# Odd mixer's entry: decays moved to GpSimd and ahead of the first MLP, input sums that scale one addend themselves, rows of values in a lasting pool

## The chip, the cores and the metric

The kernel runs on one core of one Trainium2 chip. The metric is device time in microseconds (us) of one execution, the median of several runs. Engines are called as in the profile: PE (TensorE matmul), PEld (its weight load), DVE (VectorE), ACT (ScalarE), POOL (GpSimd), SP (SyncE, which issues DMAs here).

## What is computed

Two layers of an encoder on 512 tokens of 1024 columns, float32. Layer 0 is an even mixer (windowed and neighbourhood attention) and an MLP, layer 1 an odd mixer (retention) and an MLP. Cut to what matters:

```python
def _odd_mixer(x, norm_g, w_in, dec_f, dec_b, gn_g, w_out):
    h = _rmsnorm(x, norm_g)
    q, k, v, g = _split(h @ w_in, ODD_SPLITS)
    ...
    lgf = jax.nn.log_sigmoid(dec_f.astype(jnp.float32))
    lgb = jax.nn.log_sigmoid(dec_b.astype(jnp.float32))
    y_f = _retention_dir(q, k, v, lgf, False)
    y_b = jnp.flip(_retention_dir(jnp.flip(q, 1), jnp.flip(k, 1), jnp.flip(v, 1), lgb, True), 1)
    ...  # group norm of y_f + y_b
    return (jax.nn.silu(g) * yn) @ w_out

def _mlp(x, norm_g, w1, w2):
    h = _rmsnorm(x, norm_g)
    return jnp.square(jax.nn.relu(h @ w1)) @ w2

x = x + _even_mixer(x, ...);  x = x + _mlp(x, mlp_norm[0], ...)
x = x + _odd_mixer(x, ...);   x = x + _mlp(x, mlp_norm[1], ...)
```

The retention of each of eight heads weights a pair of tokens by a decay, exp(lg * distance), where lg is the logarithm of a sigmoid of one learned number per head and direction: 16 numbers in all.

## The kernel before

Every product is made of three float32r products: each operand is split into a high part (a cast on ACT: `xh`, `whi`, `shi`, `uh`, `qh`, `ath`) and a low part (a subtraction on DVE: `xl`, `wlo`, `slo`, `ul`, `ql`, `atl`), and PE adds high-high, high-low and low-high. The activations stand transposed, eight tiles `xT[0..7]` of 128 columns of x by 512 tokens.

The stages follow each other on PE: the even mixer (to about 222 us), the first MLP, the odd mixer, the second MLP. The MLPs' products and the odd mixer's values go through a seven-product scheme (class `Strassen`, and `Values` derived from it). Before these products, `combine(i)`, four times a stage, makes four sums out of two tiles of x: both tiles are scaled by the norm's gains on ACT (tiles `y`), four DVE operations of 128x256 make the sums in a tile `c` (L1003 to L1006), ACT casts them to `uh` (L1009) and DVE subtracts to `ul` (L1010). In the odd mixer `c` has one buffer.

What sets the order: within the steps of the seven-product scheme (`stream`) the order on PE, ACT and DVE is the written one. Elsewhere, and always on POOL and SP, a scheduler in the compiler orders each engine's instructions: in program order where possible, a later instruction earlier when its inputs and its memory are there. Each engine then works in that order and waits where an input is late. Memory is taken from pools; a pool that is opened where an earlier one was closed waits for the earlier one's readers and writers.

The odd mixer's entry, in the code's order:

- `leave` (end of the first MLP): x is transposed back on PE into PSUM, ACT and DVE make the high and low parts `xh`, `xl`, and the eight tiles are copied from PSUM to `xT` (L1357), five by DVE and three by ACT.
- 25 DVE operations on 128x16 and one ACT exponential (L1588 to L1603) compute `lg` and `nlb`, the decays, from `hb`, a tile loaded in the even mixer (L520). Their tiles lie in a pool of the odd mixer. `gn` (L1606) scales the group norm's gains.
- `project` of the first quarter: q, then the four `combine` calls among k (L1679, L1684 scale them), with weights through `load_w` (L138 load, L159 high, L160 low).
- `values.stream()`: 28 steps of products (L1487 to L1489). `take`, `give`, `scale`, `centre` (L1522 to L1546) turn them into rows (tiles `s` in the pool `odd_values`, six buffers). The first quarter's rows are split at once, the other twelve are stored to DRAM on SP (L1713) and loaded again later into tiles `vr` (L1707).
- Then the pool `odd_late` is opened on the memory of the closed `odd_values`, and the heads begin: `tmp` (L1746) is the product of scores and decays, `ath` and `atl` (L1640, L1641) its parts, multiplied with the values in L1754 to L1756.

Block sums of weights come from DMAs: SP loads one block, POOL issues a second DMA that adds the other (L1064, tiles `sraw`). POOL also does a few operations of the even mixer: `qn` (L451, L456), `nb` (L751), some `wlo` (L160).

Of the kernel before, what the change touches and what calls it, by code (L numbers as in the profile page):

```python
# [9 lines left out]
F32 = mybir.dt.float32  # L10
F32R = mybir.dt.float32r
AF = mybir.ActivationFunctionType
ALU = mybir.AluOpType
# [3 lines left out]
P = 128  # L17
S = 512
# [9 lines left out]
V_ATTN, V_RET, V_MLP, V_GN, V_QA, V_KA, V_QB, V_KB = 0, 8, 16, 32, 48, 49, 50, 51  # L28
# [4 lines left out]
def hybrid_encoder_kernel(  # L33
# [18 lines left out]
    nc = tc.nc  # L52
    mm = nc.tensor.matmul
    act = nc.scalar.activation
# [37 lines left out]
    tok_ss = consts.tile([P, NB, 2], F32, name="tok_ss")  # L92
    tok_v = consts.tile([P, NB], F32, name="tok_v")
    tok_r = consts.tile([P, 2, NB], F32, name="tok_r")

    consts.tile([P, 64], F32, name="filler")


    def after(ins, before):
# [210 lines left out]
    class Norm:  # L310


        def __init__(self, vec):
            self.vec = vec
            self.xg = new_xg()

        def gain(self, d):
            return gv[:, self.vec + d : self.vec + d + 1]

        def add(self, d):  # L320
            split_gain(self.xg[d], xT[d], self.gain(d))
# [630 lines left out]
    class Strassen:  # L952
# [37 lines left out]
        def combine(self, i):  # L990

            pool, norm = self.pool, self.norm
            y = []
            for m in range(2):
                d = 2 * i + m
                t = pool.tile([P, S], F32, tag="s", bufs=self.SB, name="y")
                act(t, xT[d], AF.Copy, scale=gv[:, norm.vec + d : norm.vec + d + 1])
                y.append(t)
            b11, b12 = y[0][:, :256], y[0][:, 256:]
            b21, b22 = y[1][:, :256], y[1][:, 256:]  # L1000
            tag, bufs = self.CB
            c = pool.tile([P, 4, 256], F32, tag=tag, bufs=bufs, name="c")
            V.tensor_tensor(c[:, 0], b11, b12, op=ALU.subtract)  # L1003
            V.scalar_tensor_tensor(c[:, 1], c[:, 0], -1.0, b22, op0=ALU.mult, op1=ALU.subtract)
            V.tensor_tensor(c[:, 2], b22, b12, op=ALU.subtract)
            V.scalar_tensor_tensor(c[:, 3], c[:, 1], -1.0, b21, op0=ALU.mult, op1=ALU.subtract)  # L1006
            h = pool.tile([P, 4, 256], F32R, tag=f"uh{i}", name="uh")
            l = pool.tile([P, 4, 256], F32R, tag=f"ul{i}", name="ul")
            nc.scalar.copy(h, c)  # L1009
            V.tensor_tensor(l, c, h[:].bitcast(F32), op=ALU.subtract)  # L1010
            (xh0, xl0), (xh1, xl1) = norm.xg[2 * i], norm.xg[2 * i + 1]
            self.ins[i] = {
                "B11": (xh0[:, :256], xl0[:, :256]),
                "B21": (xh1[:, :256], xl1[:, :256]),
                "B22": (xh1[:, 256:], xl1[:, 256:]),
                "U1": (h[:, 0], l[:, 0]),
                "U2": (h[:, 1], l[:, 1]),
                "T3": (h[:, 2], l[:, 2]),
                "T4": (h[:, 3], l[:, 3]),
            }  # L1020
# [325 lines left out]
        def leave(self):  # L1346

            norm = self.next_norm()

            def split(part, ds):  # L1350
                for d in ds:
                    part(norm.xg[d], self.turned[d], norm.gain(d))

            def keep(ds, copy=V.tensor_copy):
                for d in ds:
                    xT[d] = resid.tile([P, S], F32, tag=f"xT{d}", name=f"xT{d}")
                    copy(xT[d], self.turned[d])  # L1357

            self.back(0)
            split(high_gain, range(4))  # L1360
            for d in range(2):
                split(low_gain, (d,))
                keep((d,))
            for t in (2, 3):
                self.square(t, 0, self.tmp())
            yield
            split(low_gain, (2, 3))
            for t in range(2):
                self.square(t, 1, self.tmp())
            self.back(1)  # L1370
            split(high_gain, range(4, 8))
            split(low_gain, range(4, 8))
            keep((2, 3, 4), nc.scalar.copy)
            keep((5, 6, 7))

        def scales(self):

# [64 lines left out]
    class Values(Strassen):  # L1442
# [1 line left out]

        SB = 6
        CB = ("c", 1)

        def __init__(self, pool, tiny, w, norm, done):  # L1450
            self.pool, self.tiny, self.w, self.norm, self.done = pool, tiny, w, norm, done
            self.raw, self.parts, self.ins, self.rows, self.ps = {}, {}, {}, {}, {}
            self.early, self.mid, self.post, self.asked = ({} for _ in range(4))
            self.steps = [(2, q, j, x) for q in range(2) for j in range(7) for x in range(2)]
            self.base = {(2, 0): 0, (2, 1): 14}
            self.requests()
# [113 lines left out]
                    f()  # L1570


    def odd_mixer(norm, next_norm):
        es = ExitStack()
        pool = es.enter_context(tc.tile_pool(name="odd", bufs=1))
        tiny = es.enter_context(tc.tile_pool(name="odd_tiny", bufs=1))
        tiny.tile([P, 24], F32, name="filler")
        late, marks = [], []
        scr = [None] + [dram.tile([S, S], F32, name=f"values{i}") for i in range(1, 4)]


        dx = hb[:, 8:24]
        n = 16
        lg = tiny.tile([P, n], F32, name="lg")
        u = tiny.tile([P, n], F32, name="ls_u")
        s2 = tiny.tile([P, n], F32, name="ls_s2")
        pl = tiny.tile([P, n], F32, name="ls_p")
        V.tensor_scalar(u, dx, -1.0, None, op0=ALU.mult)  # L1588
        V.tensor_tensor(u, u, dx, op=ALU.min)
        act(u, u, AF.Exp)  # L1590
        V.tensor_scalar(s2, u, 2.0, None, op0=ALU.add)
        V.reciprocal(s2, s2)
        V.tensor_tensor(u, u, s2, op=ALU.mult)
        V.tensor_tensor(s2, u, u, op=ALU.mult)
        V.tensor_scalar(pl, s2, 1.0 / 17, 1.0 / 15, op0=ALU.mult, op1=ALU.add)
        for c in (13, 11, 9, 7, 5, 3, 1):
            V.tensor_tensor(pl, pl, s2, op=ALU.mult)
            V.tensor_scalar(pl, pl, 1.0 / c, None, op0=ALU.add)
        V.tensor_tensor(pl, pl, u, op=ALU.mult)
        V.tensor_scalar(u, dx, 0.0, None, op0=ALU.min)  # L1600
        V.scalar_tensor_tensor(lg, pl, -2.0, u, op0=ALU.mult, op1=ALU.add)
        nlb = tiny.tile([P, 8], F32, name="nlb")
        V.tensor_scalar(nlb, lg[:, 8:16], -1.0, None, op0=ALU.mult)  # L1603

        gn = tiny.tile([P, 16], F32, name="gn")
        V.tensor_scalar(gn, gv[:, V_GN : V_GN + 16], -1.0 / 512, None, op0=ALU.mult)  # L1606
        gn_eps = tiny.tile([P, 1], F32, name="gn_eps")
        G.memset(gn_eps, GN_EPS)

# [33 lines left out]

        def tmp(bufs=3):
            return pool.tile([P, S], F32, tag="tmp", bufs=bufs, name="tmp")

        table = {"load": [], "exp": [], "silu": []}

# [16 lines left out]
        class Quarter:  # L1665
# [7 lines left out]
            def project(self):  # L1673
                qt = self.qt
                self.q, self.k = [None] * 2, [None] * 2

                def ev_q(m, ps):
                    t = tmp()
                    V.tensor_tensor(t, ps, rb, op=ALU.mult)  # L1679
                    self.q[m] = split(t, "q", 2)  # L1680

                def ev_k(m, ps):
                    t = tmp()
                    V.scalar_tensor_tensor(  # L1684
                        t, ps, float(np.float32(P**-0.5)), rb, op0=ALU.mult, op1=ALU.mult
                    )
                    self.k[m] = split(t, "k", 2)

                hook = None if qt else deviations
                mark = marks[-1] if qt else None  # L1690
                proj_a(w_in_o, 0, 8, qt * 256, xg, ev_q, hook)
                if qt == 0:
                    values.combine(0)
                    values.ask(-99, -2)
                    values.combine(1)
                    values.combine(2)
                    values.combine(3)
                proj_a(w_in_o, 0, 8, 1024 + qt * 256, xg, ev_k)
                if qt == 0:
                    values.scales(rc)  # L1700
                    values.ask(-2, 0)
                    values.enter()
                    return
                for t in range(NB):
                    r = late[0].tile([P, S], F32, tag="vr", bufs=4, name="vr")
                    with tc.issue_after(mark):
                        nc.scalar.dma_start(r, scr[qt][t * P : (t + 1) * P, :])  # L1707
                    self.v[t] = split(r, "v", 4)
# [110 lines left out]
        quarters = [Quarter(i) for i in range(4)]  # L1819
        with tc.tile_pool(name="odd_values", bufs=1) as first:  # L1820
            values = Values(
                first, tiny, w_in_o, norm, lambda q, t, row: quarters[q].keep_v(t, row)
            )
            quarters[0].project()
            for hl in range(2):
# [3 lines left out]
                values.stream()  # L1829
        late.append(es.enter_context(tc.tile_pool(name="odd_late", bufs=1)))  # L1830

        late[0].tile([P, 3232], F32, name="filler")
        for i in range(4):
            q, p = quarters[i], quarters[i - 1] if i else None
            n = quarters[i + 1] if i < 3 else None
# [35 lines left out]
                st.stream()  # L1871

    even_mixer(n_mlp0)
    mlp(0, n_mlp0(), n_odd)
    odd_mixer(n_odd(), n_mlp1)
    mlp(1, n_mlp1(), None)
# [79 lines left out]
```

## Time and profile before

| | |
|---|---|
| median of 3 runs | 1297.4 us (1297.08 to 1297.44) |
| profiled execution | 1296.8 us, its span 1295.0 us |
| PE / PEld busy | 1276.7 us (99%) / 1105.2 us (85%) |
| DVE / ACT / POOL busy | 1029.2 us (79%) / 818.7 us (63%) / 135.1 us (10%) |
| granted PE clock | 0.999 |
| chain that ended last | PE 88%, DVE 6%, ACT 3%, DMA 1% |

A row of a timeline has the start and the duration in us, the engine, the line, the operation, output<-inputs, shapes, and in brackets the engine's idle time before it with what ended that. A row of groups has busy us and mean ns of one, then the idle time before. A row of waits has who waited, for whom, the total, how often and the longest. Times are us from the span's start.

### The profile page before, as it was taken

What the parts mean: (1) busy time and instruction counts of PE and PEld (TensorE: products, weight loads), DVE (VectorE), ACT (ScalarE), POOL (GpSimd) and SP (SyncE); (2) the same over time, 40 slices, a digit from 0 to 9 for tenths busy, and PEclk for the clock granted to TensorE, in tenths of its full rate; (3) what the DMA queues carried; (4) which work ended last, traced back from release to release, by engine and by line L of the source; (5) the groups of instructions that cost most, each with busy time, mean ns of one, the idle gap of its engine ahead of it and who ended that gap; (6) DMA issues with size and microseconds to landing.
All of it is one profiled execution on the core that took longest, in us unless ns stands there. A gap on an engine that the chain in (4) does not pass through costs nothing.

```text
span 1295.0 us, 18645 instructions
## 1 busy us (share of the span) xinstructions
PE 1276.7 (99%) x6898; PEld 1105.2 (85%) x6898; DVE 1029.2 (79%) x1596; ACT 818.7 (63%) x1369; POOL 135.1 (10%) x136
## 2 busy tenths in 40 slices
PE   8999999999999999999999999999999999999998
PEld 7888978888989899887878888888888889898997
DVE  6788887869797988998877766856666788979888
ACT  4789875775756657586757535445357757466573
POOL 0222430010110111011000000000000111101100
PEclk9999999999999999999999999999999999999999
DMA  5323322668686787287333134132235787867852
GB/s 170 95 73 87 104 67 74 195 165 198 181 197 171 179 218 173 66 242 188 114 122 114 50 98 131 39 117 73 81 98 165 177 216 176 202 172 176 215 146 82
DMA packets 154075, 181.41 MB, mean 140 GB/s; under 512 B 11520, under 2 KB 113920, under 8 KB 153984
## 3 DMA queue, kind: packets, MB, share of 16 engines
q1 hardware_dynamic: 123344, 140.40, 34.9%
q0 software_dynamic: 23552, 33.56, 15.8%
q10 hardware_dynamic: 7088, 6.27, 1.7%
q8 instruction: 54, 0.88, 0.3%
q14 instruction: 37, 0.30, 0.1%
HBM read 173.91 MB, written 6.29 MB: 139 GB/s over the span
## 4 chain that ended last, share of the span: by engine, by line
PE 88%; DVE 6%; ACT 3%; DMA 1%; issue 1%; POOL 0%; ACTq 0%; SPq 0%; DVEq 0%
PE acc L182 9%; PE acc L180 8%; PE acc L181 8%; PE acc L1306 7%; PE acc L1307 7%; PE acc L1308 7%; PE acc L1291 5%; PE acc L1292 5%; PE acc L1293 5%; PE acc L1489 2%; PE acc L1488 1%; PE acc L1487 1%; PE aux L1754 1%; PE aux L1755 1%; PE aux L1756 1%; PE aux L1306 1%
## 5 line engine op out<-in xcount | busy, mean ns | idle before, releaser
L159 ACT CAST whi<-wraw 128x1024 fp32r<-128x1024 f32 (+2 forms) x99 | 95.4, 963 | 130.0 <-PE acc L181 92.2
L1093 ACT CAST whi<-sraw 128x1024 fp32r<-128x1024 f32 x108 | 113.2, 1050 | 76.7 <-PE acc L1308 25.0
L180 PE MATMUL acc<-xh,whi 128*128 128x512 f32 x400 | 156.4, 391 | 0.0
L181 PE MATMUL acc<-xl,whi 128*128 128x512 f32 x400 | 155.6, 389 | 0.0
L182 PE MATMUL acc<-xh,wlo 128*128 128x512 f32 x400 | 155.2, 389 | 0.0
L1099 DVE TENSOR_TENSOR wlo<-sraw,whi 128x1024 fp32r<-128x1024 f32 x108 | 131.8, 1221 | 25.0 <-ACT whi L1093 24.5
L160 DVE TENSOR_TENSOR wlo<-wraw,whi 128x1024 fp32r<-128x1024 f32 (+2 forms) x90 | 102.2, 1136 | 52.8 <-ACT whi L159 51.7
L1064 POOL DMA_DIRECT2D sraw<-in_w_mlp_out_dram x32 | 38.6, 1221 | 705.7 <-DMA sraw<-in_w_mlp_out_dram 495.9
L182 PEld LDWEIGHTS acc<-xh,wlo 128*128 128x128 f32 x400 | 75.1, 188 | 15.8
L180 PEld LDWEIGHTS acc<-xh,whi 128*128 128x128 f32 x400 | 75.1, 188 | 15.7 <-ACT whi L159 0.4
L181 PEld LDWEIGHTS acc<-xl,whi 128*128 128x128 f32 x400 | 75.1, 188 | 15.4
L1093 ACT CAST shi<-sraw 128x1024 fp32r<-128x1024 f32 x52 | 54.6, 1050 | 33.8 <-PE acc L1308 10.7
L1291 PE MATMUL acc<-uh,whi 128*128 128x256 f32 x256 | 73.0, 285 | 0.1
L1260 DVE SCALAR_TENSOR_TENSOR rows<-acc,tok_r,rows 128x512 f32<-128x512 f32 (+1 forms) x97 | 71.3, 739 | 1.9 <-PE acc L1308 1.9
L1292 PE MATMUL acc<-ul,whi 128*128 128x256 f32 x256 | 72.4, 283 | 0.0
L1293 PE MATMUL acc<-uh,wlo 128*128 128x256 f32 x256 | 72.4, 283 | 0.0
L1099 DVE TENSOR_TENSOR slo<-sraw,shi 128x1024 fp32r<-128x1024 f32 x52 | 63.5, 1221 | 9.7 <-ACT shi L1093 9.5
L1099 DVE TENSOR_TENSOR wlo<-wraw,whi 128x1024 fp32r<-128x1024 f32 x40 | 48.8, 1220 | 12.9 <-ACT whi L1093 12.9
L204 PE MATMUL acc<-whi,xh 128*128 128x384 f32 (+1 forms) x160 | 52.7, 331 | 0.0
L205 PE MATMUL acc<-wlo,xh 128*128 128x384 f32 (+1 forms) x160 | 52.5, 328 | 0.0
L206 PE MATMUL acc<-whi,xl 128*128 128x384 f32 (+1 forms) x160 | 52.3, 327 | 0.0
L1291 PEld LDWEIGHTS acc<-uh,whi 128*128 128x128 f32 x256 | 49.1, 192 | 1.0 <-ACT s L1182 1.0
(393 smaller groups left out, 3924.7 us busy)
## 6 DMA issues: line engine op xcount, KB each, us to landing
sraw<-in_w_mlp_out_dram SPq DMA_DIRECT2D x48, 512.0 KB
wraw<-in_w_mlp_in_dram SPq DMA_DIRECT2D x40, 512.0 KB
wraw<-in_w_in_o_dram SPq DMA_DIRECT2D x40, 512.0 KB
sraw<-in_w_mlp_in_dram SPq DMA_DIRECT2D x36, 512.0 KB
sraw<-in_w_mlp_out_dram POOLq DMA_DIRECT2D x32, 512.0 KB, 8.6
wraw<-in_w_mlp_out_dram SPq DMA_DIRECT2D x32, 512.0 KB
sraw<-in_w_mlp_in_dram POOLq DMA_DIRECT2D x24, 512.0 KB, 8.4
wraw<-in_w_out_o_dram SPq DMA_DIRECT2D x16, 512.0 KB
```

The costliest lines, as they stand in the source:

```text
L159: nc.scalar.copy(hu, used)
L160: eng.tensor_tensor(lu, used, hu.bitcast(F32), op=ALU.subtract)
L180: mm(ps[m], hi[:, k % 4, cs], xh, start=k == 0, stop=False)
L181: mm(ps[m], hi[:, k % 4, cs], xl, start=False, stop=False)
L182: mm(ps[m], lo[:, k % 4, cs], xh, start=False, stop=k == nk - 1)
L1093: nc.scalar.copy(h, self.weight(k))
L1099: V.tensor_tensor(l, self.weight(k), h.bitcast(F32), op=ALU.subtract)
L1291: mm(o, h[:, i, cs], bh, start=st, stop=False, skip_group_check=True)
L1292: mm(o, h[:, i, cs], bl, start=False, stop=False, skip_group_check=True)
L1293: mm(o, l[:, i, cs], bh, start=False, stop=i == 3, skip_group_check=True)
L1306: mm(oc, bh[:, i, cs], hc, start=st, stop=False, skip_group_check=True)
L1307: mm(oc, bh[:, i, cs], lc, start=False, stop=False, skip_group_check=True)
```

## The change

The decays are computed in a function of their own, called between the even mixer and the first MLP, with 23 operations on POOL, three on DVE and one on ACT; their tiles lie in the pool that is open from the start. `gn` is made on POOL. `leave` copies columns 2 to 7 by ACT and 0 and 1 by DVE. `combine` scales one of the two tiles on ACT; the other is read as it is, and three of the four sums multiply it by the gain or by its negative (`ngv`, made at the start on POOL). Rows of values, the scaled tile and the reloaded rows share one tag `row` with six buffers in the odd mixer's own pool. This holds for all three uses of `combine`, except that the MLPs take the tile from their own tag. Filler tiles change their sizes with it.

```diff
+    ngv = consts.tile([P, 32], F32, name="ngv")
+    G.tensor_scalar(ngv, gv[:, :32], -1.0, None, op0=ALU.mult)
+    lg = consts.tile([P, 16], F32, name="lg")
+    nlb = consts.tile([P, 8], F32, name="nlb")
+    ls = [consts.tile([P, 16], F32, name=f"ls{i}") for i in range(3)]
...
         def combine(self, i):
-            y = []
-            for m in range(2):
-                d = 2 * i + m
-                t = pool.tile([P, S], F32, tag="s", bufs=self.SB, name="y")
-                act(t, xT[d], AF.Copy, scale=gv[:, norm.vec + d : norm.vec + d + 1])
-                y.append(t)
-            b11, b12 = y[0][:, :256], y[0][:, 256:]
-            b21, b22 = y[1][:, :256], y[1][:, 256:]
+            y = self.tmp()
+            act(y, xT[2 * i], AF.Copy, scale=norm.gain(2 * i))
+            b11, b12 = y[:, :256], y[:, 256:]
+            x21, x22 = xT[2 * i + 1][:, :256], xT[2 * i + 1][:, 256:]
+            g, ng = norm.gain(2 * i + 1), norm.minus_gain(2 * i + 1)
...
             V.tensor_tensor(c[:, 0], b11, b12, op=ALU.subtract)
-            V.scalar_tensor_tensor(c[:, 1], c[:, 0], -1.0, b22, op0=ALU.mult, op1=ALU.subtract)
-            V.tensor_tensor(c[:, 2], b22, b12, op=ALU.subtract)
-            V.scalar_tensor_tensor(c[:, 3], c[:, 1], -1.0, b21, op0=ALU.mult, op1=ALU.subtract)
+            V.scalar_tensor_tensor(c[:, 1], x22, ng, c[:, 0], op0=ALU.mult, op1=ALU.subtract)
+            V.scalar_tensor_tensor(c[:, 2], x22, g, b12, op0=ALU.mult, op1=ALU.subtract)
+            V.scalar_tensor_tensor(c[:, 3], x21, ng, c[:, 1], op0=ALU.mult, op1=ALU.subtract)
...
-            keep((2, 3, 4), nc.scalar.copy)
-            keep((5, 6, 7))
+            keep(range(2, 8), nc.scalar.copy)
...
+    def decays():
+        dx = hb[:, 8:24]
+        u, s2, pl = ls
+        G.tensor_scalar(u, dx, -1.0, None, op0=ALU.mult)
+        V.tensor_tensor(u, u, dx, op=ALU.min)
+        act(u, u, AF.Exp)
+        G.tensor_scalar(s2, u, 2.0, None, op0=ALU.add)
+        V.reciprocal(s2, s2)
+        G.tensor_tensor(u, u, s2, op=ALU.mult)
+        G.tensor_tensor(s2, u, u, op=ALU.mult)
+        G.tensor_scalar(pl, s2, 1.0 / 17, 1.0 / 15, op0=ALU.mult, op1=ALU.add)
+        for c in (13, 11, 9, 7, 5, 3, 1):
+            G.tensor_tensor(pl, pl, s2, op=ALU.mult)
+            G.tensor_scalar(pl, pl, 1.0 / c, None, op0=ALU.add)
+        G.tensor_tensor(pl, pl, u, op=ALU.mult)
+        V.tensor_scalar(u, dx, 0.0, None, op0=ALU.min)
+        G.tensor_scalar(pl, pl, -2.0, None, op0=ALU.mult)
+        G.tensor_tensor(lg, pl, u, op=ALU.add)
+        G.tensor_scalar(nlb, lg[:, 8:16], -1.0, None, op0=ALU.mult)
...
     def odd_mixer(norm, next_norm):
...
-        V.tensor_scalar(gn, gv[:, V_GN : V_GN + 16], -1.0 / 512, None, op0=ALU.mult)
+        G.tensor_scalar(gn, gv[:, V_GN : V_GN + 16], -1.0 / 512, None, op0=ALU.mult)
...
+        def row():
+            return pool.tile([P, S], F32, tag="row", bufs=6, name="row")
...
-                    r = late[0].tile([P, S], F32, tag="vr", bufs=4, name="vr")
+                    r = row()
...
-                first, tiny, w_in_o, norm, lambda q, t, row: quarters[q].keep_v(t, row)
+                first, row, tiny, w_in_o, norm, lambda q, t, row: quarters[q].keep_v(t, row)
...
-        late[0].tile([P, 3232], F32, name="filler")
+        late[0].tile([P, 2048], F32, name="filler")
...
     even_mixer(n_mlp0)
+    decays()
     mlp(0, n_mlp0(), n_odd)
     odd_mixer(n_odd(), n_mlp1)
```

More of the change, by code (lines that the diff above doesn't have):

```diff
@@ L94, in hybrid_encoder_kernel @@
     tok_r = consts.tile([P, 2, NB], F32, name="tok_r")
-    consts.tile([P, 64], F32, name="filler")
+    ngv = consts.tile([P, 32], F32, name="ngv")
[3 more added lines that the diff above has]
+    ls = [consts.tile([P, 16], F32, name=f"ls{i}") for i in range(3)]
+    consts.tile([P, 88], F32, name="filler")
     def after(ins, before):
@@ L318, in gain, with minus_gain @@
             return gv[:, self.vec + d : self.vec + d + 1]
+        def minus_gain(self, d):
+            return ngv[:, self.vec + d : self.vec + d + 1]
         def add(self, d):
@@ L1442, in hybrid_encoder_kernel, with __init__ @@
     class Values(Strassen):
-        SB = 6
         CB = ("c", 1)
-        def __init__(self, pool, tiny, w, norm, done):
+        def __init__(self, pool, row, tiny, w, norm, done):
             self.pool, self.tiny, self.w, self.norm, self.done = pool, tiny, w, norm, done
+            self.tmp = row
             self.raw, self.parts, self.ins, self.rows, self.ps = {}, {}, {}, {}, {}
@@ L1576, in odd_mixer @@
         tiny = es.enter_context(tc.tile_pool(name="odd_tiny", bufs=1))
-        tiny.tile([P, 24], F32, name="filler")
+        tiny.tile([P, 32], F32, name="filler")
         late, marks = [], []
         scr = [None] + [dram.tile([S, S], F32, name=f"values{i}") for i in range(1, 4)]
[L1582 to L1603, printed above, removed]
         gn = tiny.tile([P, 16], F32, name="gn")
-        V.tensor_scalar(gn, gv[:, V_GN : V_GN + 16], -1.0 / 512, None, op0=ALU.mult)
+        G.tensor_scalar(gn, gv[:, V_GN : V_GN + 16], -1.0 / 512, None, op0=ALU.mult)
         gn_eps = tiny.tile([P, 1], F32, name="gn_eps")
```

## The prediction

> **What bounds the kernel now.** I read the page's share lines first, then a table of busy times by stage, then what the tensor engine waited for in each stage, and last the timelines around the waits.
>
> ```profile
> PE 1276.7 (99%) x6898; PEld 1105.2 (85%) x6898; DVE 1029.2 (79%) x1596; ACT 818.7 (63%) x1369; POOL 135.1 (10%) x136
> ...
> 20.00:120.00 100.00, 96.52 (x558) 86.63 (x557) 81.74 (x217) 79.66 (x191) 21.18 (x20) 1.00 0.29 82
> 222.00:262.00 40.00, 40.00 (x186) 33.40 (x185) 31.79 (x51) 30.77 (x54) 2.58 (x2) 1.00 0.63 179
> 562.00:574.00 12.00, 12.00 (x56) 9.94 (x55) 11.83 (x43) 9.62 (x16) 2.27 (x2) 1.00 1.07 288
> 585.00:592.00 7.00, 5.03 (x21) 3.26 (x20) 6.26 (x7) 5.10 (x7) 1.20 (x1) 1.00 0.56 156
> ```
>
> The columns after the stretch are PE, PEld, DVE, ACT and POOL busy time, granted clock, DMA share and GB/s. PE is busy for 99% of the span at full clock, so only a stretch where PE stands still can give time back. The entry of the first MLP (222 to 262) has no idle PE at all: what the change saves there is worth nothing. The odd mixer's entry has a full DVE (11.83 of 12 us from 562) and, from 585 on, 1.97 us of idle PE.
>
> ```profile
> PE acc L1488 <- DVE slo L1099: 1.1, 1, 1.1
> PE acc L1489 <- DVE ul L1010: 0.9, 1, 0.9
> PE aux L1754 <- ACT ath L1640: 1.9, 1, 1.9
> ```
>
> These are all of PE's waits from 555 to 700: two on DVE at the entry, one on ACT when the values end. Their size, from the start times:
>
> ```profile
> 585.31 0.40 PE L1487 MATMUL acc<-shi,uh 128*128 128x512 f32 x1
> 586.77 0.50 PE L1488 MATMUL acc<-slo,uh 128*128 128x512 f32 x1 [1.06 <-DVE slo L1099]
> ...
> 589.04 0.50 PE L1489 MATMUL acc<-shi,ul 128*128 128x512 f32 x1 [0.91 <-DVE ul L1010]
> 589.38 0.39 PE L1487 MATMUL acc<-shi,uh 128*128 128x512 f32 x1
> 589.61 0.39 PE L1488 MATMUL acc<-slo,uh 128*128 128x512 f32 x1
> ...
> 663.47 0.39 PE L180 MATMUL acc<-xh,whi 128*128 128x512 f32 x1
> 665.78 0.73 PE L1754 MATMUL aux<-ath,vh 128*128 128x512 f32 x2 [1.92 <-ACT ath L1640]
> ```
>
> Matmuls start 0.23 us apart (589.38, 589.61). From 585.31 to 589.38 six of them started, which takes 1.38 at that pace and took 4.07: 2.69 us lost. From 663.47 to 665.78 one started: 2.31 - 0.23 = 2.08 us lost. Together 4.77 us, and that is nearly all that this change can win.
>
> **The change part by part.** *DVE's queue at the odd entry.* Removed are 25 tiny operations of the decays, the scaling of gn, and the copies of columns 5 to 7 of x; the sums of the inputs keep their number.
>
> ```profile
> 558.47 0.68 DVE L1357 COPY xT<-aux 128x512 f32<-128x512 f32 x1
> ...
> 560.26 0.16 DVE L1589 TENSOR_TENSOR ls_u<-ls_u,hb 128x16 f32<-128x16 f32 x1
> ...
> 563.05 0.17 DVE L1593 TENSOR_TENSOR ls_u<-ls_u,ls_s 128x16 f32<-128x16 f32 x1
> 563.13 0.15 DVE L114 TENSOR_TENSOR rq_t<-tok_v,rq_r 128x4 f32<-128x4 f32 x1
> ...
> 566.07 0.18 DVE L1598 TENSOR_SCALAR ls_p<-ls_p 128x16 f32<-128x16 f32 x1
> 566.28 0.17 DVE L1597 TENSOR_TENSOR ls_p<-ls_p,ls_s 128x16 f32<-128x16 f32 x1
> ...
> 566.79 1.22 DVE L1010 TENSOR_TENSOR ul<-c,uh 128x1024 fp32r<-128x1024 f32 x1
> ```
>
> The copies take 558.47 to 560.26, 1.79 us. A tiny operation beside independent work holds DVE for 0.08 (563.05 to 563.13), one directly behind its own input for 0.21 (566.07 to 566.28). Of the 25 that follow 560.26 (24 of the decays and gn), 20 go at the short price, 20 x 0.085 = 1.7, and five at the long one. Those five stand ahead of the ul at 566.79, which has to wait for ACT's uh anyway:
>
> ```profile
> 565.40 1.03 ACT L1009 CAST uh<-c 128x1024 fp32r<-128x1024 f32 x1
> ```
>
> uh ends at 566.43, so taking the five away wins 566.79 - 566.43 = 0.36, not 1.05. The gross saving on DVE is 1.79 + 1.7 + 0.36 = 3.85 us.
>
> Against it stands what the sums now do themselves. Three of four take a gain from a column of memory in place of a number or none:
>
> ```profile
> L303 DVE SCALAR_TENSOR_TENSOR xl<-aux,gv,xh 128x512 fp32r<-128x512 f32 x3 | 2.1, 743 | 0.4 <-ACT xh L299 0.4
> L1684 DVE SCALAR_TENSOR_TENSOR tmp<-acc,rstd_b 128x512 f32<-128x512 f32 x2 | 1.4, 684 | 0.0
> ```
>
> With a column of gains 743 ns, with a number 684: 0.06 more. Twelve operations make 0.7 us. (Bounds: 0 if the fixed part is hidden, 0.7 if not; I take 0.7.) Net 3.85 - 0.7 = 3.1 us less ahead of the last ul, the one that PE's wait at 589.04 names. PE needs it 2.69 us earlier, the slo in front of it 1.23 earlier. So both waits go, with 0.4 us to spare; I take 2.6 of the 2.69. If the spare is not there, the left-over shows as a wait on the same ul; the bounds of this term are 1.2 (the slo's wait alone) and 2.7.
>
> *ACT at the odd entry.* It takes three more copies and drops four of eight scalings of x.
>
> ```profile
> L997 ACT ACTIVATE y<-xT,gv 128x512 f32<-128x512 f32 x8 | 5.3, 710 | 0.0
> L1357 ACT COPY xT<-aux 128x512 f32<-128x512 f32 x3 | 1.6, 641 | 0.0
> ...
> 559.84 1.06 ACT L159 CAST whi<-wraw 128x1024 fp32r<-128x1024 f32 x1 [0.86 <-PE acc L181]
> ```
>
> Three copies add 1.6, four scalings take away 2.65: ACT is lighter by 1 us over the stage. The copies come first, however: they would run until about 560.6, so the whi at 559.84, which stood idle for 0.86 us before, is 0.7 late at the most. What waits for it is the k projection, behind some 5 us of q matmuls. Nothing on PE's path: 0, with 0.3 late as the upper bound.
>
> *The rows of values.* In the kernel before they lie in the pool of the value stage, and the attention weights (ath) lie in the pool opened after it.
>
> ```profile
> 658.47 0.20 ACT L1536 ACTIVATION_READ_ACCUMULATOR s<-acc,vscale 128x1 f32 x1
> 665.11 1.66 ACT L1640 CAST ath<-tmp 128x512 fp32r<-128x512 f32 x3 [6.43 <-DMA values<-s]
> ...
> 658.23 0.69 DVE L1746 TENSOR_TENSOR tmp<-aux,strip 128x512 f32<-128x512 f32 x1
> ```
>
> ACT is free at 658.67 and the input of ath, tmp, is ready at 658.92, but ath starts at 665.11: it waits for the last store of rows, because the memory of the closed pool is given out only when all of it is free. In the changed kernel the rows stay in a pool that lives on; the other tenants of the closed pool are last read by products that stand on PE ahead of the one that filled tmp's input. Then ath starts near 659.0, 6 us sooner, and PE, which has other matmuls until 663.7, does not wait. Gain 2.08; I take 2.1. The nearest thing late next is the atl behind it on DVE, four times (0.68 + 0.68) from 658.2, done by 663.7, in step with PE: bounds 1.5 and 2.1. The reloads of rows now share six buffers with the stores; they come a whole head stage after the last store, so 0.
>
> *The decays in their new place.* Their tiles now live from the start, so the earliest moment is the landing of hb.
>
> ```profile
> 34.14 0.17 DVE L538 TENSOR_SCALAR nsink<-hb 128x8 f32<-128x8 f32 x1 [2.64 <-DMA hb<-in_heads_dram]
> ...
> 39.98 0.62 POOL L456 TENSOR_TENSOR qn<-raw,rs 128x256 f32<-128x256 f32 x1 [37.92 <-DVE rs L117]
> ...
> L751 POOL TENSOR_TENSOR nb<-mask,rpbt 128x192 f32<-128x192 f32 x16 | 10.5, 658 | 34.6 <-DVE nm L557 22.1 <-DMA wraw<-in_w_out_e_dram 4.0 <-PE aux L774 3.2
> L751 POOL TENSOR_TENSOR nb<-mask,rpbt 128x256 f32<-128x256 f32 x8 | 6.0, 751 | 3.4 <-DMA rpbt<-in_rpb_dram 2.0 <-DVE nm L557 1.4
> L160 POOL TENSOR_TENSOR wlo<-wraw,whi 128x1024 fp32r<-128x1024 f32 x2 | 4.8, 2401 | 16.5 <-ACT whi L159 16.5
> ...
> 243.52 2.58 POOL L1064 DMA_DIRECT2D sraw<-in_w_mlp_out_dram  x2 [35.44 <-DVE kept L1146]
> ```
>
> No row has a 128x16 operation on POOL. From 256 to 1024 columns the time grows by 1650 ns, 2.15 ns a column; 751 less 240 x 2.15 is 0.24 us, my estimate, between nothing and the 0.66 of 192 columns. 23 operations make 5.4 us, with about 2 us for the hops to DVE (three operations), ACT (one) and back. Starting at 34.1 they end near 41.5, some 1.5 us behind the qn at 39.98 if all stand ahead of it on POOL; PE then has projection matmuls to do, which it was busy with. Placed at the first MLP's entry instead, the chain has the 35 idle us before the issue at 243.52 to itself. I charge 0.3 us (bounds 0 and 11, the latter from 0.66 an operation). The four DVE and ACT operations go beside softmax work that has gaps. ngv falls into the 37.92 idle us before qn: 0. gn is one operation ahead of POOL's issues at the odd entry: 0 to 0.66 us later for a weight sum that is used some 15 us on, so 0.
>
> Sum against the profiled execution's 1296.8: 2.6 + 2.1 - 0.3 = 4.4, which gives 1292.4. The median of the runs is 0.6 higher, 1297.4, and the same step gives 1293.0.
>
> **Rule and row.** What POOL does to DVE shows in one place:
>
> ```profile
> 53.48 0.16 DVE L642 TENSOR_TENSOR sm<-sm,es 128x4 f32<-128x4 f32 x1
> ...
> 60.70 1.84 POOL L160 TENSOR_TENSOR wlo<-wraw,whi 128x768 fp32r<-128x768 f32 x1 [15.35 <-ACT whi L159]
> 61.30 1.27 DVE L642 TENSOR_TENSOR sm<-sm,es 128x4 f32<-128x4 f32 x1
> ```
>
> The same DVE operation takes 0.16 us alone and 1.27 when it begins inside a POOL operation, and ends with it (62.57 and 62.54). [...]
>
> **Rivals.** (1) *POOL's chain blocks the even mixer* (slower): DVE and ACT are 80% busy there and PE already loses 3.5 us from 20 to 120. If all 23 operations hold up qn, the delay is 34.1 + 2 + 23x - 40.0; at x = 0.38 us an operation it eats the 4.7 won and from there decides; at 0.66 it is 11.3 us, 1297.4 - 4.7 + 11.3 = 1304.0. Against it: the estimate is 0.24. 0.09. [...] 0.08. (3) *The entry's wait only changes its cause*: the c tile has one buffer, so sum, cast and subtraction of the four inputs run strictly one after another, and shifted DVE work need not help them; or ACT's copies come to matter. Then the first term gives 0 to 1.2: 1297.4 - 2.1 - 0.6 + 0.3 = 1295.0. 0.16. (4) *The change doesn't free ath*: another tenant of the closed pool or a store still gates it; only the first term is left: 1297.4 - 2.6 + 0.3 = 1295.1. Against it: the wait names the store of rows alone. 0.06. (5) Neither stall goes: 1297.4. 0.03.
>
> **How the numbers follow.** The forecast, both stalls gone, has what is left, 0.58, own range 1291.9 to 1294.6. A difference of 0.2% (2.6 us, so 1294.8 and 1300.0) is about what a measurement tells from none. Faster: 0.58, half of (3) and (4), a quarter of (2): 0.71. Slower: 0.07 of rival (1)'s 0.09. Same: the rest, 0.22. The range takes in (2), (3), (4) and (5): 1291.5 to 1297.6; out of it are (1) and a gain over 5.9.
>
> **What would show it.** Right: in the entry DVE has idle time before 589 and PE no wait on ul; ath starts within 1 us of its tmp; the tiny operations are gone from 555 to 575 and stand on POOL with 0.15 to 0.35 us each; PE's busy share in 585 to 592 is full. Wrong: a new PE wait in 34 to 60 on qn or on p; DVE operations of 0.16 stretched beside POOL; ath still behind a DMA; the last ul behind uh on ACT; a different order of matmuls with waits that weren't there.

## The result, and the profile after

The changed kernel takes 1305.0 us (median of 4 runs, 1303.8 to 1306.3) against 1297.4 for the kernel before beside it: ratio 1.0056, 95% interval 1.0042 to 1.0071. It is slower, where 1293.0 was forecast. In the sessions of the experiments the median of the kernel before was 1297.0 to 1298.7, on one and the same chip too (1297.9 and 1298.6), so the experiments below go by their ratio to the kernel before that was timed beside them. Where that difference comes from is told in the section on the hardware.

The page of the changed kernel, its table by stage (the stretches that correspond to those shown of before; the odd entry comes 4.3 us later), and what PE waited for in the whole kernel (the longest) and from 555 to 700:

```profile
PE 1280.7 (98%) x6898; PEld 1107.6 (85%) x6898; DVE 1027.2 (79%) x1570; ACT 813.2 (62%) x1360; POOL 142.0 (11%) x161
```

```profile
20.00:120.00 100.00, 92.51 (x526) 83.12 (x524) 76.27 (x203) 74.53 (x181) 26.58 (x43) 0.98 0.28 79
...
566.00:578.00 12.00, 12.00 (x56) 9.92 (x55) 11.77 (x24) 7.94 (x11) 1.92 (x3) 1.00 1.07 279
589.00:596.00 7.00, 4.05 (x12) 2.48 (x12) 7.00 (x7) 4.11 (x5) 1.19 (x1) 0.86 0.48 150
```

```profile
PE aux L635 <- DVE qk L485: 3.7, 1, 3.7
...
PE acc L1493 <- DVE slo L1105: 2.0, 1, 2.0
PE acc L1494 <- DVE ul L1016: 1.0, 1, 1.0
```

PE starts 526 matmuls from 20 to 120 where it started 558, and has a wait of 3.7 us there that was not there before. The two waits of the odd entry, forecast to go, have grown from 1.1 and 0.9 to 2.0 and 1.0, and the granted clock falls there to 0.86. The wait of PE for ath is gone.

Both kernels start the same number of matmuls (6898), so the n-th start of the one can be set against the n-th of the other. This table, worked out from the start times, shows how many us later than in the kernel before the n-th matmul starts; the last three columns are experiments told of below.

| matmul | at (us, before) | changed kernel | own tile | copies back | three repairs |
|---|---|---|---|---|---|
| 200 | 46 | -0.4 | +0.7 | +0.4 | +0.2 |
| 500, even mixer | 100 | +4.2 | +0.9 | +6.2 | +0.3 |
| 3200, before the odd entry | 556 | +4.3 | +0.9 | +6.3 | +0.3 |
| 3600, behind the entry | 651 | +6.5 | +4.3 | +4.5 | -2.6 |
| 3700, first heads | 676 | +4.5 | +2.3 | +2.5 | -4.9 |
| 5000, end of the heads | 972 | +7.0 | +4.7 | +5.1 | -5.0 |
| 6800 | 1270 | +7.0 | +4.7 | +5.1 | -5.0 |

So there are four separate effects: 4.6 us lost in the even mixer, 2.2 lost at the odd entry (where 2.6 were to be won), 2.0 won at ath, 2.5 lost slowly over the 300 us of the heads. Every column is one execution; how far a stage's loss varies from one to the next with the same code is told under the even mixer.

**The even mixer.** POOL, DVE and PE of the changed kernel around the new wait:

```profile
39.91 0.25 POOL L1591 TENSOR_SCALAR ls<-ls 128x16 f32<-128x16 f32 x1
40.24 0.62 POOL L465 TENSOR_TENSOR qn<-raw,rs 128x256 f32<-128x256 f32 x1
...
44.81 0.62 POOL L465 TENSOR_TENSOR qn<-raw,rs 128x256 f32<-128x256 f32 x1
45.39 0.23 POOL L1590 TENSOR_TENSOR ls<-ls,ls 128x16 f32<-128x16 f32 x1
...
47.97 0.22 POOL L1592 TENSOR_TENSOR ls<-ls,ls 128x16 f32<-128x16 f32 x1
```

```profile
48.23 0.17 DVE L1593 TENSOR_SCALAR ls<-hb 128x16 f32<-128x16 f32 x1 [4.15 <-POOL ls L1592]
48.35 0.48 DVE L566 CUSTOM_DVE_ANT_0 p<-aux,dist,nsink 128x256 f32<-128x256 f32 x1
...
48.87 1.53 DVE L485 SCALAR_TENSOR_TENSOR qk<-aux,gq,qk 64x512 fp32r<-64x512 f32 x2
```

```profile
46.56 0.34 PE L212 MATMUL acc<-whi,xl 128*128 128x384 f32 x1
50.55 0.36 PE L635 MATMUL aux<-qk 128*128 128x256 f32 x1 [3.65 <-DVE qk L485]
```

L1593 is `V.tensor_scalar(u, dx, 0.0, None, op0=ALU.min)`. It writes over `u`, which POOL's L1592 (`pl * u`), at the end of the chain, has yet to read. POOL paused its chain at 40.16 for two kinds of attention work (qn and a wlo) and came back at 45.39. DVE stood 4.15 us before an operation of 0.17 us, with the scores (L566, from 48.35) and the low parts of q and k (L485, from 48.87; the expectation of experiment 1 calls them squares) queued behind it, and PE behind those. After PE's wait the clock is down, as the windows show, before first, then the changed kernel:

```profile
52.00:58.00 6.00, 6.00 (x36) 5.35 (x36) 5.18 (x15) 5.95 (x16) 0.00 (x0) 1.00 0.31 82
```

```profile
52.00:58.00 6.00, 6.00 (x29) 6.00 (x28) 3.82 (x13) 3.68 (x12) 0.00 (x0) 0.77 0.26 68
```

PE is busy all the time in both, but at a granted clock of 0.77 it starts 29 matmuls and not 36. The clock's own record in the trace has it at half for 3.41 us, from 51.38 on, and at full on both sides. Matmuls of 512 columns start 0.43 us apart at half clock (594.39 and 594.82 in the rows of the odd entry below) and 0.23 at full. How much idle time went before the falls of this case is told in the last section.

The stall is the same each time, its price is not. Five of the experiments below have the changed kernel's code up to the odd entry, and in all of them PE waits 3.6 to 3.7 us here. In the changed kernel and two of them (the first and third of experiment 4) the clock was then at half for 3.41 us, and 4.2 to 5.2 us were lost by matmul 500; in the other three (experiments 2 and 3 and the second of 4) it was at half for 6.83 us, and 6.2 to 7.0 were lost.

**The odd entry.** ACT, DVE and PE of the changed kernel:

```profile
561.66 1.60 ACT L1363 COPY xT<-aux 128x512 f32<-128x512 f32 x3
...
563.07 0.67 ACT L1363 COPY xT<-aux 128x512 f32<-128x512 f32 x1
563.55 1.17 ACT L1363 COPY xT<-acc 128x512 f32<-128x512 f32 x2
...
564.61 1.15 ACT L165 CAST whi<-wraw 128x1024 fp32r<-128x1024 f32 x1
...
571.61 1.05 ACT L1015 CAST uh<-c 128x1024 fp32r<-128x1024 f32 x1
```

```profile
565.79 1.22 DVE L166 TENSOR_TENSOR wlo<-wraw,whi 128x1024 fp32r<-128x1024 f32 x1 [2.10 <-ACT whi L165]
...
579.35 1.23 DVE L1016 TENSOR_TENSOR ul<-c,uh 128x1024 fp32r<-128x1024 f32 x1 [1.12 <-ACT uh L1015]
...
585.98 1.23 DVE L1016 TENSOR_TENSOR ul<-c,uh 128x1024 fp32r<-128x1024 f32 x1 [0.58 <-ACT uh L1015]
...
590.38 1.22 DVE L1105 TENSOR_TENSOR slo<-sraw,shi 128x1024 fp32r<-128x1024 f32 x1
```

```profile
589.28 0.40 PE L1492 MATMUL acc<-shi,uh 128*128 128x512 f32 x1
591.65 0.50 PE L1493 MATMUL acc<-slo,uh 128*128 128x512 f32 x1 [1.98 <-DVE slo L1105]
...
593.92 0.67 PE L1494 MATMUL acc<-shi,ul 128*128 128x512 f32 x1 [0.96 <-DVE ul L1016]
594.39 0.63 PE L1492 MATMUL acc<-shi,uh 128*128 128x512 f32 x1
594.82 0.63 PE L1493 MATMUL acc<-slo,uh 128*128 128x512 f32 x1
```

Six copies hold ACT from 561.66 to 564.7. Less 4.29, the lateness at matmul 3200, whi stands at 560.32 (559.84 before), but uh at 567.32 (565.40 before), 1.9 later. DVE now has the room that was forecast, and spends it waiting for ACT: 2.10 for whi, 1.12 and 0.58 for uh. The slo and ul that PE wants come at the end of that row, and from 593.92 on the matmuls stand some 0.43 apart: the clock is at half from 594.10 to 597.51.

**ath** begins at once behind its tmp, which ends at 665.39, and PE has no wait there:

```profile
665.48 0.62 ACT L1641 CAST ath<-tmp 128x512 fp32r<-128x512 f32 x1 [0.34 <-DVE tmp L1750]
```

**The heads.** Groups of matmuls from 684 to 980, before first, then the changed kernel (count, busy us, mean ns of one):

```profile
L180 PE MATMUL acc<-xh,whi 128*128 128x512 f32 x229 | 89.1, 389 | 0.0
L181 PE MATMUL acc<-zl,whi 128*128 128x512 f32 x128 | 49.8, 389 | 0.0
```

```profile
L186 PE MATMUL acc<-xh,whi 128*128 128x512 f32 x224 | 87.2, 389 | 0.0
L187 PE MATMUL acc<-zl,whi 128*128 128x512 f32 x128 | 50.5, 395 | 0.0
```

Products of x and weights are as fast as ever; those that read z (and ath) take some 5 ns more. By the start times too: with z they follow each other in 232 ns and not 227, with ath in 232 and not 228.5. 528 of them (three times 128 and three times 48) make 2.6 us, and 2.5 were lost. Nothing in the arithmetic differs. What does is where these tiles lie in each partition's memory: the filler that comes before them went from 3232 to 2048 columns, and the pool of z and ath begins at 384 bytes modulo 512 in the kernel before, at 0 in the changed one, while weights and x are at 384 in both (addresses of the built programs).

### The profile page after: what moved, and what is told of

The parts are those of the page before. It is cut to its first block, busy times and chain, and to the rows that moved or that the text cites. A ratio compares the mean times of both kernels' runs of the same rounds, so it can differ in the third digit from the quotient of the medians.

```text
span 1302.0 us, 18630 instructions
## 1 busy us (share of the span) xinstructions
PE 1280.7 (98%) x6898; PEld 1107.6 (85%) x6898; DVE 1027.2 (79%) x1570; ACT 813.2 (62%) x1360; POOL 142.0 (11%) x161
## 4 chain that ended last, share of the span: by engine, by line
PE 90%; DVE 4%; ACT 3%; issue 1%; DMA 1%; POOL 1%; SPq 0%; ACTq 0%; DVEq 0%; POOLq 0%
PE acc L186 9%; PE acc L187 9%; PE acc L188 9%; PE acc L1312 7%; PE acc L1313 7%; PE acc L1314 7%; PE acc L1297 5%; PE acc L1299 5%; PE acc L1298 5%; PE acc L1494 2%; PE acc L1492 2%; PE acc L1493 2%; PE aux L1758 1%; PE aux L1759 1%; PE aux L1760 1%; PE aux L1312 1%
## 5 line engine op out<-in xcount | busy, mean ns | idle before, releaser
L187 PE MATMUL acc<-zl,whi 128*128 128x512 f32 x128 | 50.5, 395 | 0.0
```

The costliest lines, as they stand in the source:

```text
L187: mm(ps[m], hi[:, k % 4, cs], xl, start=False, stop=False)
```

## The experiments

Ratios are to the kernel before on the same chip. The last three columns of the table above are experiments 1, 2 and the first of 8.

**1. The minimum in a tile of its own.**

```diff
-        u, s2, pl = ls
+        u, s2, pl, mn = ls
...
-        V.tensor_scalar(u, dx, 0.0, None, op0=ALU.min)
+        V.tensor_scalar(mn, dx, 0.0, None, op0=ALU.min)
...
-        G.tensor_tensor(lg, pl, u, op=ALU.add)
+        G.tensor_tensor(lg, pl, mn, op=ALU.add)
```

`ls` has four tiles for it, and the filler behind them is as much shorter, so nothing else moves.

> The changed kernel, but the minimum of dx and 0 gets a tile of its own instead of overwriting u, which POOL still has to read. Theory (the reused tile): that DVE operation waited 4.15 us for POOL's chain with the scores and the squares of q and k queued behind it, PE stood for 3.65 us, and the clock fell after it; so DVE no longer waits for POOL at 48 us, PE's wait at 50.5 and the clock's fall go, and the kernel takes 4.2 us less than the changed one: 1300.8 us. Rival (the chain as such: qn late on POOL, or DVE and POOL holding each other up): the wait stays or moves to qn, 1304 to 1305 us.

Measured 1300.7 us, ratio 1.0019 (1.0010 to 1.0028), 0.37% off the changed kernel's. The operation now goes first of all, and the clock stays up:

```profile
33.93 0.19 DVE L1593 TENSOR_SCALAR ls<-hb 128x16 f32<-128x16 f32 x1
```

```profile
46.00:52.00 6.00, 5.90 (x37) 5.34 (x36) 5.60 (x14) 4.49 (x11) 3.92 (x13) 1.00 0.50 134
52.00:58.00 6.00, 6.00 (x37) 5.38 (x37) 4.51 (x14) 5.87 (x16) 0.00 (x0) 1.00 0.29 78
```

POOL still has 3.92 us of its work from 46 to 52, and PE is as busy as before. What cost most of the 4.6 us was one tile used twice, not the chain. What is left of the chain's price is 0.3 to 1.0 us by the profiles of the four kernels that have it without the reuse, where 0.3 was charged. PE has two waits for qn on POOL there, 0.5 us together, which the kernel before does not have from 20 to 120. In this profile 3.3 us are won in the even mixer, but 3.3 are lost at the odd entry, where the changed kernel's lost 2.2 with the same waits: the clock was at half for 6.83 us there and not for 3.41.

**2. Three columns copied by DVE again.**

```diff
-            keep(range(2, 8), nc.scalar.copy)
+            keep((2, 3, 4), nc.scalar.copy)
+            keep((5, 6, 7))
```

> The changed kernel with columns 5 to 7 of x copied by DVE again, as before. Theory A (ACT's three copies and what they push back, the first whi by some 1.9 us and with it uh, are the odd entry's bound): the two waits of PE at 589 and 592 (3.1 us) and the fall of the clock after them go in part or whole: 2.5 to 4.5 us less, 1300.5 to 1302.5 us. Theory B (the one buffer of c, sum, cast and subtraction strictly in turn): the entry keeps its waits, 1304 to 1305.5 us.

Measured 1300.5 us, ratio 1.0015 (1.0006 to 1.0024). From matmul 3200 to 3600 this kernel wins 1.8 us on the kernel before, where the changed kernel lost 2.2: 4.0 us for three copies. (The 6.2 us before that are the even mixer's, told above.) PE's waits from 555 to 700 are down to one:

```profile
PE acc L1494 <- DVE slo L1105: 0.3, 1, 0.3
```

That is theory A, the copies on ACT. Its reverse, the kernel before with these three copies on ACT and nothing else:

> The kernel before with columns 5 to 7 copied by ACT and nothing else. Prediction's step (b): nothing on PE's path, while DVE has 1.8 us less: 1296.0 to 1297.4 us. Theory A (the copies push whi, the scalings of x and uh back by 1.9 us, and the chain through c with them): the entry's stall grows by 1 to 2 us, with a fall of the clock behind it 2 to 4: 1298.5 to 1301.5 us.

Measured ratio 1.0023 (1.0013 to 1.0032): 3 us slower, although DVE has 1.8 us less to do. The longest of PE's waits from 555 to 620 are now on ul and uh:

```profile
PE acc L1488 <- DVE ul L1010: 1.6, 1, 1.6
PE acc L1486 <- ACT uh L1009: 0.7, 1, 0.7
```

PE's waits there add up to 3.2 us, 1.2 more than before; the rest of what this execution loses lies in the clock, which was at half for 6.83 us behind them and for 3.41 behind the wait for ath.

**3. Two buffers for c.** (`CB = ("c", 2)`, and five `sraw` buffers in place of six.)

> The changed kernel with two buffers for c in the odd mixer, paid for with five buffers of weight sums in place of six. Theory B (the one buffer of c bounds the entry): sums of the next input run while ACT casts the one before, ul waits for uh no more, PE's waits at 589 and 592 go: 2.5 to 4.5 us less, 1300.5 to 1302.5 us. Theory A (ACT's copies are the bound): no gain, 1304 to 1306 us, the fifth buffer costing up to 1 us where a load comes later.

Measured ratio 1.0061 (1.0049 to 1.0074), no gain. The waits of ul for uh are gone, as theory B has it, but the scheduler now puts the sums of two inputs ahead together, and the first slo late (at 586.66 on DVE):

```profile
587.93 0.80 PE L1493 MATMUL acc<-slo,xh 128*128 128x512 f32 x1 [3.84 <-DVE slo L1105]
```

So this run does not clear the one buffer; it says that with ACT as it is, room in c alone does not help, since the order changes with it. What the sixth `sraw` buffer is worth was not told apart.

**4. Where the pools lie.** Three changes of fillers, nothing else.

```diff
# 384 bytes further on (values' and heads' pools)
-        tiny.tile([P, 32], F32, name="filler")
+        tiny.tile([P, 128], F32, name="filler")
# 128 bytes further on
+        tiny.tile([P, 64], F32, name="filler")
# everything at a multiple of 256: the lasting pool too
-    consts.tile([P, 88], F32, name="filler")
+    consts.tile([P, 120], F32, name="filler")
+        tiny.tile([P, 64], F32, name="filler")
```

> The changed kernel with a filler of 128 columns in place of 32 in the small odd pool, so that everything in the pools of the values and of the heads lies 384 bytes further on: the same offset modulo 512 bytes as the weights and x, as it was in the kernel before for the heads' pool. Theory (placement): matmuls whose two operands lie at different offsets modulo 512 start about 5 ns further apart; from 684 us on that cost 2.5 us, which goes, and the values' own 430 products gain 0.5 us besides: 1302.0 us, range 1301.3 to 1302.7. Rival (the slow matmuls come from what runs beside them, DMA or DVE): no change, 1305.0 us.

> The changed kernel with the pools of the values and heads 128 bytes further on: their offset modulo 512 bytes is 128, that of the weights and of x stays 384. Theory (a matmul starts later when its two operands lie at different offsets modulo 512): slow matmuls as in the changed kernel, 1305.0 us, range 1304.3 to 1305.7. Rival (offset 0 itself is bad, or only the step of 128 counts): the tail is fast, 1301 to 1302.5.

> The changed kernel with every large tile, the weights and x too, at a multiple of 256 bytes (a filler of the lasting pool 128 bytes longer, one of the small odd pool too); the pools of values and heads then lie 256 bytes off the weights modulo 512, but at the same offset modulo 256. Theory (what counts is that a matmul's two operands share their offset modulo 256): heads' and values' products are fast, as with 128 bytes more in those pools alone, and nothing else changes: ratio to the kernel before 1.001 to 1.003, 1299 to 1301.5 us. Rival 1 (a multiple of 256 is bad in itself): all 6898 matmuls some 5 ns slower, over 1320 us. Rival 2 (it goes by 512): as the changed kernel, 1304 to 1306 us.

Ratios: 384 bytes 1.0018 (1.0009 to 1.0026), 128 bytes 1.0012 (1.0003 to 1.0021), all at multiples of 256 1.0031 (1.0019 to 1.0044). The first gained more than the 3.0 us expected: 4.9 by the ratios, 3.9 by the start times. The first could not tell a modulus from another; the second refuted 512, as it was fast at 128 against 384; the third kept the offset between the operands at 256 modulo 512 and was fast again, with nothing else slowed. The rows of the heads in the third:

```profile
L186 PE MATMUL acc<-xh,whi 128*128 128x512 f32 x227 | 88.3, 389 | 0.0
L188 PE MATMUL acc<-zh,wlo 128*128 128x512 f32 x128 | 49.9, 390 | 0.0
```

From matmul 3700 to 5000 each of the first two gains 0.1 us on the kernel before and the third loses 0.3, where the changed kernel lost 2.5. In all three the values' stage gains 0.9 us too (3400 to 3600). Its pool lies at 256 modulo 512 in the kernel before and at 0 in the changed one, and in both it has slow and fast products side by side. Weights of the lasting pools (whi) with u in the values' pool, from 600 to 660, in the kernel before and then in the third:

```profile
L1487 PE MATMUL acc<-whi,uh 128*128 128x512 f32 x32 | 12.6, 395 | 0.0
```

```profile
L1492 PE MATMUL acc<-whi,uh 128*128 128x512 f32 x37 | 14.4, 389 | 0.0
```

By the start times of the kernel before, these weights follow each other in 233 ns with u and in 229 with x, which is at 384 as they are; weights in the values' pool (shi) do the reverse, 229 with u and 232 with x. So neither a place nor a tile is slow by itself. In these runs a matmul is some 5 ns slower (395 ns against 389 in the groups) when its two operands lie at different offsets modulo 256 bytes; both at 128 or both at 0 is the same (389 and 390 in the heads). Only offsets that differ by a multiple of 128 were run.

**5. Rows in the lasting pool alone**, in the kernel before, with the offsets modulo 512 kept.

> The kernel before with the lasting pool for rows of values alone (scaled tiles of x, rows and reloaded rows in one tag of six buffers), operands at the same offsets modulo 512 bytes as before. Prediction's step (c): ath starts behind its tmp and not behind the last store, 2.1 us less: 1295.3 us, range 1295.0 to 1295.9. Rival: the gain is given back within the heads, as reloads share six buffers with nothing behind them: 1297.4.

Measured ratio 0.9986 (0.9977 to 0.9995), 1.8 us. By the start times, matmuls 3600 to 3700 win 2.1 us, none is given back later, and 1.6 are lost at the odd entry, where the change does nothing to PE's waits: the two are the same to 0.1 us, as are the busy times of PE, but the clock is not (the kernel before first, from 585 to 606):

```profile
585.00:606.00 21.00, 19.03 (x81) 14.61 (x80) 16.29 (x18) 13.08 (x19) 2.41 (x2) 1.00 0.74 185
```

```profile
585.00:606.00 21.00, 19.03 (x74) 14.48 (x73) 15.07 (x16) 12.01 (x17) 2.41 (x2) 0.92 0.68 167
```

The same two waits, 2.0 us in all, are followed by a fallen clock in one execution and not in the other.

**6. The decays alone** (own tile, on POOL ahead of the first MLP), in the kernel before.

> The kernel before with the decays alone moved to POOL ahead of the first MLP, the minimum in a tile of its own; gn and the copies stay on DVE. Even mixer: 0.9 us later, as the changed kernel with the tile of its own showed. Odd entry: DVE has 2.1 us less ahead of the last ul, of which the two waits (2.69 us in all) give up 1.5 to 2.1. Net 0.6 to 1.2 less: 1296.2 to 1296.8 us. Rival (the entry is bound by ACT and the chain through c, not by DVE's work): nothing gained there, 1298.3 us.

Measured ratio 0.9982 (0.9973 to 0.9991), 2.3 us; by the profile 1.0 is lost in the even mixer and 1.3 won at the entry, where the slo's wait of 1.1 is gone and ul's 0.9 stays. The profiled execution has only 0.3 won in all. What the median adds goes with the clock: the eleven executions of this kernel ran at a mean granted clock of 0.998 or more (1295.0 to 1297.2 us), while of the 21 of the kernel before beside it eleven ran at 0.997 (1298.6 to 1300.0) and ten at 0.998 or more (1296.6 to 1297.8). Against those ten this kernel's median is 0.9 us ahead, that of experiment 5 0.5.

**7. The sums alone**, in the kernel before.

> The kernel before with the input sums alone changed (one addend scaled by the sums themselves, in all three stages that have them). By the prediction's own terms DVE gets 0.06 us for each of twelve sums, 0.7 us, onto a full stretch ahead of the last ul, so PE's wait grows by as much: 1298.1 us. Rival (ACT, 2.65 us lighter, has uh and shi sooner, and the chain sum, cast, subtraction starts sooner): up to 1 us less, 1296.4 us.

Measured ratio 1.0032 (1.0020 to 1.0045), 4.2 us slower. The waits at the entry:

```profile
PE acc L1490 <- DVE slo L1101: 1.5, 1, 1.5
PE acc L1491 <- DVE ul L1012: 1.4, 1, 1.4
PE acc L1489 <- ACT uh L1011: 0.7, 1, 0.7
```

They are 1.6 us more than before for 0.8 us more work on DVE (some 480 ns a sum against 418, twelve times), and the clock falls behind them (at half for 6.83 us) and again behind the wait for ath at 668, which was there before without a fall. I had the sign and the first term right and left the clock out.

**8. The three repairs together** (1, 2 and the 384 bytes), and the same with the old sums.

> The changed kernel with three repairs at once: a tile of its own for the minimum, columns 5 to 7 copied by DVE, and the pools of the values and heads 384 bytes further on. If the three losses are separate, their gains add. Each by the matmuls' start times in its own run: 4.3 us in the even mixer, 4.0 at the odd entry, 4.1 in the values and heads, 12.4 off the changed kernel's 1305.0 makes 1292.6 us, range 1291.5 to 1294. If they share a cause (say, the clock), less comes together: 1295 to 1297.

> The version with the three repairs, but with the input sums of the kernel before (both tiles scaled on ACT). The sums alone, put into the kernel before, made it 4.2 us slower. If that loss is the sums' own, this version is faster than the three repairs: 1290.5 to 1291.3 us, limited by the 0.9 us that PE still loses at the entry there. Rival (the sums cost only on a DVE that is full, and there the decays' leaving has made room, while ACT needs the 2.65 us that the sums spare it): no difference or up to 1 us slower, 1291.9 to 1293.

Measured 1291.9 us, ratio 0.9950 (0.9938 to 0.9963), and 1292.7 us, 0.9951 (0.9939 to 0.9964). Both are faster than either kernel, by 0.5% on the one before, and the three gains nearly add: 0.37, 0.38 and 0.41% one by one make 1.16, together they make 1.06, with 0.09 to 0.15 of uncertainty on each ratio. All that PE still waits for from 555 to 700 in the first:

```profile
PE acc L1494 <- DVE slo L1105: 0.4, 1, 0.4
PE acc L1494 <- DVE wlo L1105: 0.2, 1, 0.2
```

Between old and new sums there is no difference clear of the noise: with the decays off DVE and the copies back on it, the sums' 0.8 us does not show. If anything the new sums are ahead: PE's two waits at the entry are 0.9 and 0.3 us with the old ones, and by the start times the whole gain is 3.8 us with the old and 5.0 with the new.

## Why the prediction was wrong, and where it was right

- *The decays in their new place, charged 0.3.* Wrong by 4.3 us. POOL's operations were sized fairly (estimate 0.24 us, measured 0.20 to 0.32; but in the chain they start 0.29 to 0.36 apart, so 23 take some 7.4 us and not 5.4), and qn, on which rival (1) had put the danger, came 0.3 us later than before (40.24 and 39.98). The step that failed is the sentence that the four DVE and ACT operations "go beside softmax work that has gaps". It priced them by their length. It did not ask what each waits for, that one waits for a *reader* on POOL because a tile is used twice, and what stands behind it on DVE. Rival (1) had the right engine and the wrong victim; that its 1304.0 lies so near the measured 1305.0 is chance.
- *ACT at the odd entry, 0 with 0.3 as the upper bound.* Wrong by 4.0 us with the other parts in, some 3.8 alone (matmuls 3200 to 3600 of the kernel with the copies alone; 3.0 by the medians). Of the 3.8, 1.2 are longer waits; the rest goes with the fallen clock. That whi would be up to 0.7 late was right (0.5). I asked who waits for whi, and not for what else ACT does behind the copies: the scalings of x, uh and shi, on the chain from which slo and ul come. Rival (3) named this ("or ACT's copies come to matter") and gave it 0 to 1.2 gained, not 2.2 lost, since it left PE's stall as it was and did not let it grow.
- *DVE's queue at the odd entry, 2.6 of 2.69 won.* Not in the changed kernel, for the reason above. Where the copies were back on DVE it came to 1.8 and, in the three repairs, 2.1 (matmuls 3200 to 3400). DVE's relief was real, but of the 3.1 us it was credited with, 1.8 were the copies, moved to an engine on which they cost more.
- *Rows of values, 2.1 won.* Right: 2.0 in the changed kernel, 2.1 alone, ath 0.1 us behind its tmp's end, and the reloads cost nothing.
- *Fillers.* No step spoke of them, though the change has three new sizes: a cost of 2.5 us taken as nothing without a reason.
- *Rival (2), which has 0.08 of the chances.* No run shows that each of POOL's operations holds DVE up once: beside POOL's chain, from 37.6 to 38.8, DVE's five operations of 128x16 and 128x24 took 0.18 to 0.23 us in the changed kernel, and 0.18 in the kernel before (38.99 to 39.93).
- *The clock.* The sum took it as 1.00 throughout, as the profile before had it; that this profile had no fall at the odd entry was, by the clocks told of in the last section, likely chance. In the changed kernel each stall of some 3 us and more (3.65; 1.98 and 0.96 together) brought a fall beside the stall itself: 1.2 us in the even mixer (seven starts fewer from 52 to 58), 1.6 at the entry (eight starts of 0.43 us in place of 0.23).

## What to carry to other kernels

When operations move to another place in an engine's queue, ask for each what it waits for, write-after-read on a reused scratch tile included, and who queues behind it; its own duration says nothing of its price. Work taken from a full engine is only won if the engine that gets it is not on the same chain: see what stands behind it there, not only what reads it. When a change shifts addresses, check that the two operands of the hot matmuls still lie at the same offset modulo 256 bytes (2.5 us over the heads here). And before a stall is priced from one profile, look at the granted clock of the other executions: the profiled one may be the one in which it stayed up.

## What the runs showed of the hardware that was not expected

A float32r matmul of 128x512 takes some 5 ns more, 2% of the 227 from one start to the next, when its operands differ by 128 bytes in their offset modulo 256 (395 ns against 389 in the groups).

Two waits of PE within 4 us that total 2.0 us were followed by half the clock in one execution and not in another (experiment 5 and the kernel before); the wait for ath, 1.9 to 2.1 us, was followed by a fall in two of the four profiles that have it. After waits that come to 2.9 us and more within 5 us (2.9 and 3.65 in the changed kernel, 3.8 in experiment 3) it fell in each profile looked at. The clock's record in the 14 traces shows where the falls lie: every fall begins a whole multiple of 3.41 us behind the clock's first rise (in the changed kernel 12, 171 and, at the program's end, 378 times 3.413 behind it) and, but for those at a program's end, lasts 3.41 or 6.83 us. So it may count how a stall lies against this grid; that is the author's reading, and no run tested it alone. In experiment 5 most of the two waits lies in one stretch of it, 586.07 to 589.48, in which PE was busy for 1.94 us, and the clock was at half from 589.48 on. In the kernel before they are divided between two stretches, with a border at 586.95 and PE busy for 2.35 and 2.51 us, and nothing follows. In the changed kernel the stretches ahead of its two falls had PE busy for 0.83 us (47.96 to 51.38) and 1.48 (590.69 to 594.10). Where the limit lies is not shown: in the kernel before and in experiment 6 the stretch with the wait for ath had PE busy for 1.81 and 1.67 us and no fall behind it.

The kernel before shows two such kinds of execution in its times. Of its 79 executions beside the experiments 40 ran at a mean granted clock of 0.998 or more, in 1296.3 to 1298.0 us, and 39 at 0.997, in 1298.4 to 1300.7. That the latter had their fall at the odd entry is likely but not shown, as none of them has a profile on record. The median moves with the share of the two kinds, and so do the ratios: the four executions beside the result, 1297.1 to 1297.5, are by their times of the first kind.

And POOL's gn, 16 columns, took as long as the DVE operation beside it (the rows are of the changed kernel, and like operations of POOL alone take 0.25):

```profile
559.60 1.29 POOL L1607 TENSOR_SCALAR gn<-gv 128x16 f32<-128x16 f32 x1 [43.87 <-PE acc L1345]
```

```profile
559.56 1.22 DVE L166 TENSOR_TENSOR wlo<-wraw,whi 128x1024 fp32r<-128x1024 f32 x1
```

They end 0.11 us apart, at 560.89 and 560.78. It was POOL that took longer: the changed kernel's wlo operations of this shape on DVE take 1.22 us throughout from 540 to 600 (eleven of them). Nothing waited for gn.
